# Walking the columns of the 256-column products in runs of four: two transformer blocks on one Trainium2 core

## The chip, the cores and the metric

The kernel runs on one core of one Trainium2 chip, in one launch. The metric is the device time of an execution in microseconds. Times are medians of runs; the profile is one further execution, and its own time stands beside its span in the table below.

## The reference, cut to what matters

The input is one sequence of 512 tokens with 1024 features, float32. A first block has an FFN, a token mixer (four mLSTM and four HGRN2 heads between an input projection `w_in` and an output projection) and a second FFN. A second block has a gated-linear-attention layer (GLA) and a differential-attention layer, each followed by an MLP. Every sublayer normalises its input over the features, scales and shifts it by vectors made from a condition vector, and adds its gated output to the residual `h`.

```python
def swiglu(y, w_gate, w_up, w_down):
    return (jax.nn.silu(y @ w_gate) * (y @ w_up)) @ w_down
...
y = rmsnorm(h, mix_pre_g[l]) * (1.0 + sc2) + sh2
y = token_mix(y, w_in[l], mlstm_conv_w[l], ...)
h = h + g2 * rmsnorm(y, mix_post_g[l])
...
y = jnp.square(jax.nn.relu(h @ mlp_w1[i])) @ mlp_w2[i]
x = x + gate_c * y
```

All of the large work is matrix products of 512 tokens with weights of 1024 to 4096 columns.

## The kernel before, in words

**Products.** Each operand is split into a high and a low part of type fp32r, and a product is the sum of three matmuls per 128 rows of the contraction: high by high, high by low, low by high. `fm` (L378) puts the weights into the array and streams X, so that its result has features on the partitions: lines L387 (high by high), L388 (reads the low part of X) and L389. `tm` (L394) puts X into the array and streams weights; its result has tokens on the partitions: lines L405 to L407. Both take their streamed operand and their result through `runs` (L374). For 512 columns it walks them as four passes over 32 places that lie 16 elements (64 bytes) apart, four elements at each place; for any other width it leaves them as they are.

**X.** The input X of a sublayer has eight row tiles of 128 features, each with a high and a low part of 512 tokens. Two row tiles, four parts, lie in one buffer (in the instruction order `XAr0_2048_103`, `XAr2048_2048_104`, `XAr4096_2048_105`, `XAr6144_2048_106`, and XB likewise). `to_X` (L467) makes one half of the tokens: for each of the four buffers PE transposes four blocks of `y` (L474), ACT scales and shifts them (L482, in the profile line L118), and DVE writes the high part (L486) and the low part (L487). `y` comes from `scaled_to` (DVE L460, and ACT), behind the root of the mean square (POOL L428).

**Halved stages.** In five places, at the start of a sublayer, the first products are made for tokens 0 to 255 and then for 256 to 511 (HALVES): twice in `fm_split` (L830; the mixer, first stage here, and GLA, third), three times at the start of `ffn` (L601; the second FFN, second stage here, and the two MLPs, fourth and fifth). A product there has 256 columns and 24 matmuls. Per half there are 4 products in `fm_split`, 6 in `ffn`. The first half of X is complete when the stage begins. The second is made during it: `flush` (L572) is called inside `fm` when a set number of products (`due`) has been recorded, 2 in `fm_split`, 5 or 4 in `ffn`, and writes the steps of `to_X` there, so that the first half's other products stand behind them in the program. The transposes are tied behind the last product recorded (`behind`).

```python
        if len(products) == due[0]:
            flush((1, 1, 1, 1))
...
            hi, lo = (X.groups[kp][:, i:i + 3:2, hs] for i in range(2))
            V.tensor_copy(hi, v2)
            V.tensor_tensor(lo, v2, hi.bitcast(F32), op=ALU.subtract)
```

**Order.** Each engine runs its instructions in the order that a scheduler fixes when the program is built. It works from the dependences that it finds between the places which instructions read and write, and puts in the waits between engines.

**Background.** The vectors of the condition are worked out on DVE (L247, L251) between the rest; weights come on SP's queue and are split by ACT (L338, in the profile L118) and DVE (L341). In `last_half` (L543), at the end, the last piece of the last row block is made as two `tm` products of 256 columns.

Of the kernel before, what the change touches and what calls it, by code (L numbers as in the profile page):

```python
# [35 lines left out]
def kernel(ctx: ExitStack, tc: tile.TileContext, a: dict, out: bass.AP):  # L36
# [336 lines left out]

    def runs(ap):  # L374

        return ap.rearrange("p (a b c) -> p b a c", b=4, c=4) if ap.shape[1] == 512 else ap

    def fm(p, wt, X, span, c=0):  # L378

        s, n = span  # L380
        kn = wt.shape[2]
        work(0.65 * kn * n / 512)
        for k in range(kn):
            xh, xl = X[k]
            wh, wl = wt[:, 0, k, c:c + 128], wt[:, 1, k, c:c + 128]
            xh, xl = runs(xh[:, s:s + n]), runs(xl[:, s:s + n])
            PE.matmul(runs(p), lhsT=wh, rhs=xh, start=k == 0, stop=False)  # L387
            PE.matmul(runs(p), lhsT=wh, rhs=xl, start=False, stop=False)  # L388
            done = PE.matmul(runs(p), lhsT=wl, rhs=xh, start=False, stop=k == kn - 1)  # L389
        products.append(done)  # L390
        if len(products) == due[0]:
            flush((1, 1, 1, 1))
# [1299 lines left out]
```

## Time and profile before

| | |
|---|---|
| median of 3 runs | 2275.97 us (2275.53 to 2278.2) |
| profiled execution, its own time | 2276.14 us |
| its span | 2274.4 us |
| mean granted clock of TensorE | 0.997 of 2.4 GHz |
| PE busy | 2222.1 us (98%) |
| DVE, ACT, POOL busy | 1396.7, 923.7, 189.5 us |

The span goes from the first to the last instruction of the profiled execution; its own time is 1.7 us longer. PE's busy time counts a matmul from its start to its modelled end; neighbours overlap, so that the pace of matmuls is read from their starts or their number in a window. PEld is the weight load of a matmul. A window's row gives, per engine, the busy time and the number of instructions in it, then the granted clock of TensorE. In a timeline row, the brackets tell how long the engine had been idle and what released it.

### The profile page before, as it was taken

To read this page: it belongs to the slowest core of one execution; us is meant where nothing else is said; L and a number is where in the kernel's file an instruction comes from. 1 tells how busy PE (TensorE), PEld (TensorE's weight loads), DVE (VectorE), ACT (ScalarE), POOL (GpSimd) and SP (SyncE) were. 2 spreads that over 40 slices of the span, in tenths; PEclk is the share of its full clock that TensorE was granted. 3 is DMA by queue.
4 is the path that set the end of the run, shared out by engine and by line. 5 is a ranking of instruction groups with operands and counts; after the bars stand their busy time and mean duration, and the time that the engine had idled before them with its cause. 6 is when DMAs were issued, how large, how long until landed. Compare 5 with 4: busy or idle time off the path is not lost.

```text
span 2274.4 us, 27957 instructions
## 1 busy us (share of the span) xinstructions
PE 2222.1 (98%) x10904; PEld 1837.6 (81%) x10904; DVE 1396.7 (61%) x2371; ACT 923.7 (41%) x1722; POOL 189.5 (8%) x126
## 2 busy tenths in 40 slices
PE   6999999999899999999999999999999999999998
PEld 4888887888788888888888888888886767988887
DVE  7856555765777745545644775666756577634465
ACT  4332224644665332224644443222445456433223
POOL 0111121000101111100010011101000110100000
PEclk9999999999999999999999999999999999999999
DMA  9755444445323644542332255454331321423221
GB/s 274 245 177 179 163 158 71 106 107 107 102 75 110 207 165 167 176 139 66 125 125 91 72 176 185 158 164 142 129 124 58 116 65 57 157 93 102 93 94 64
DMA packets 212900, 294.69 MB, mean 130 GB/s; under 512 B 7257, under 2 KB 120328, under 8 KB 212768
## 3 DMA queue, kind: packets, MB, share of 16 engines
q1 hardware_dynamic: 212128, 291.85, 41.4%
q8 instruction: 85, 1.39, 0.2%
q10 hardware_dynamic: 640, 1.07, 0.1%
q14 instruction: 47, 0.39, 0.1%
HBM read 290.78 MB, written 2.11 MB: 129 GB/s over the span
## 4 chain that ended last, share of the span: by engine, by line
PE 88%; DVE 5%; ACT 4%; issue 2%; POOL 1%; DMA 1%; POOLq 0%; ACTq 0%; DVEq 0%
PE PS L407 13%; PE PS L405 13%; PE PS L387 13%; PE PS L388 13%; PE PS L406 13%; PE PS L389 13%; PE PS L1498 1%; ACT RS L118 1%; DVE w L341 1%; POOL sm L428 1%; PE PS L924 1%; PE PS L1527 1%; ACT tmp L118 1%; ACT w L118 1%; DVE h L513 1%
## 5 line engine op out<-in xcount | busy, mean ns | idle before, releaser
L341 DVE TENSOR_TENSOR w<-raw,w 128x1024 fp32r<-128x1024 f32 (+1 forms) x392 | 459.9, 1177 | 405.3 <-ACT w L118 400.9
L118 ACT ACTIVATE w<-raw 128x1024 fp32r<-128x1024 f32 (+1 forms) x392 | 389.2, 1000 | 493.6 <-PE PS L407 275.8
L388 PE MATMUL PS<-XAr,w 128*128 128x512 f32 (+1 forms) x1328 | 482.2, 364 | 0.6 <-DVE XAr L713 0.5
L389 PE MATMUL PS<-XAr,w 128*128 128x512 f32 (+1 forms) x1328 | 481.0, 363 | 0.0
L387 PE MATMUL PS<-XAr,w 128*128 128x512 f32 (+1 forms) x1328 | 479.7, 365 | 0.0
L405 PE MATMUL PS<-w,XAr 128*128 128x512 f32 x806 | 313.4, 389 | 1.0 <-DVE XAr L850 0.8
L406 PE MATMUL PS<-w,XAr 128*128 128x512 f32 x806 | 311.2, 386 | 0.0
L407 PE MATMUL PS<-w,XAr 128*128 128x512 f32 x806 | 309.9, 385 | 0.0
L388 PEld LDWEIGHTS PS<-XAr,w 128*128 128x128 f32 x1328 | 250.0, 188 | 40.2 <-DVE XAr L713 1.3
L387 PEld LDWEIGHTS PS<-XAr,w 128*128 128x128 f32 x1328 | 249.5, 188 | 40.4 <-ACT XAr L118 1.4
L389 PEld LDWEIGHTS PS<-XAr,w 128*128 128x128 f32 x1328 | 250.0, 188 | 38.4
L407 PE MATMUL PS<-w,XBr 128*128 128x512 f32 x704 | 274.5, 390 | 0.5 <-DVE XBr L850 0.5
L406 PE MATMUL PS<-w,XBr 128*128 128x512 f32 x704 | 274.3, 390 | 0.0
L405 PE MATMUL PS<-w,XBr 128*128 128x512 f32 x704 | 274.2, 390 | 0.1
L118 ACT ACTIVATE tmp<-PS 128x512 f32<-128x512 f32 (+3 forms) x227 | 104.5, 466 | 407.3 <-PE PS L389 321.5
L251 DVE SCALAR_TENSOR_TENSOR acc<-araw,silu_c,acc 128x512 f32<-128x512 f32 x266 | 199.1, 748 | 40.9 <-DMA araw<-in_ada_w_dram 37.9
L261 POOL PARTITION_ALL_REDUCE tmp<-acc x38 | 131.3, 3456 | 942.9 <-DVE acc L251 791.8
L405 PEld LDWEIGHTS PS<-w,XAr 128*128 128x128 f32 x806 | 151.3, 188 | 30.3 <-DVE XAr L850 1.0
L407 PEld LDWEIGHTS PS<-w,XAr 128*128 128x128 f32 x806 | 151.2, 188 | 29.8 <-issue 0.8
L406 PEld LDWEIGHTS PS<-w,XAr 128*128 128x128 f32 x806 | 151.3, 188 | 29.0 <-issue 1.6
L405 PEld LDWEIGHTS PS<-w,XBr 128*128 128x128 f32 x704 | 131.8, 188 | 29.4 <-ACT RS L118 0.5
L406 PEld LDWEIGHTS PS<-w,XBr 128*128 128x128 f32 x704 | 132.0, 188 | 29.0 <-DVE w L341 1.0
(293 smaller groups left out, 2486.8 us busy)
## 6 DMA issues: line engine op xcount, KB each, us to landing
araw<-in_ada_w_dram SPq DMA_DIRECT2D x152, 512.0 KB
raw<-in_mlp_w_dram SPq DMA_DIRECT2D x56, 1024.0 KB
raw<-in_ffn_w_gate_dram SPq DMA_DIRECT2D x20, 1024.0 KB
raw<-in_ffn_w_up_dram SPq DMA_DIRECT2D x20, 1024.0 KB
raw<-in_ffn_w_down_dram SPq DMA_DIRECT2D x20, 1024.0 KB
raw<-in_w_in_dram SPq DMA_DIRECT2D x16, 1024.0 KB
raw<-in_gla_w_in_dram SPq DMA_DIRECT2D x12, 1024.0 KB
raw<-in_diff_w_in_dram SPq DMA_DIRECT2D x12, 1024.0 KB
```

What stands on the lines that cost most here:

```text
L118: ins = S.activation(out, in_, func, **kw)
L251: i = V.scalar_tensor_tensor(acc, raw[:, k, :], col, acc, op0=ALU.mult, op1=ALU.add)
L261: G.partition_all_reduce(red, acc, channels=128, reduce_op=bass_isa.ReduceOp.add)
L341: ins = V.tensor_tensor(wt[:, 1, ks], src[:, ks], wt[:, 0, ks].bitcast(F32), op=ALU.subtract)
L387: PE.matmul(runs(p), lhsT=wh, rhs=xh, start=k == 0, stop=False)
L388: PE.matmul(runs(p), lhsT=wh, rhs=xl, start=False, stop=False)
L389: done = PE.matmul(runs(p), lhsT=wl, rhs=xh, start=False, stop=k == kn - 1)
L405: PE.matmul(runs(p), lhsT=xh[:, s:s + 128], rhs=wh, start=n == 0, stop=False)
L406: PE.matmul(runs(p), lhsT=xh[:, s:s + 128], rhs=wl, start=False, stop=False)
L407: done = PE.matmul(runs(p), lhsT=xl[:, s:s + 128], rhs=wh, start=False, stop=n == last)
L428: G.tensor_tensor(r, ms, mhalf[:, 0:w], op=ALU.pow)
L513: V.scalar_tensor_tensor(h[:, blk, C2[c]], y[blk][:, C2[c]], r[:, b:b + 1], h[:, blk, C2[c]], op0=ALU.mult, op1=ALU.add)
```

## The change

`runs` now walks operands and results of 256 columns too: four passes over 16 places, 64 bytes apart, four elements at each.

```diff
     def runs(ap):
 
-        return ap.rearrange("p (a b c) -> p b a c", b=4, c=4) if ap.shape[1] == 512 else ap
+        return ap.rearrange("p (a b c) -> p b a c", b=4, c=4) if ap.shape[1] >= 256 else ap
```

It is reached by the products of the five halved stages, and by the two of 256 columns in `last_half`. The scheduled order changes with it in the five stages.

First place: PE, first halved stage, where the second half's transposes (L474) are followed by the rest. `w_2787` and `w_2792` hold the weights of the third and fourth product of the first half; `waits DVE_49` is a wait for DVE. Before, the third product is over and the fourth is three quarters through:

```order
L389 MATMUL PS_70<-XAr4096_2048_105,w_2792 128x256 [waits DVE_49]
L387 MATMUL PS_70<-XAr4096_2048_105,w_2792 128x256
L388 MATMUL PS_70<-XAr4096_2048_105,w_2792 128x256
L389 MATMUL PS_70<-XAr4096_2048_105,w_2792 128x256
L474 MATMUL PS_70<-ident_113,Y_111 128x128 [waits DVE_49]
L474 MATMUL PS_70<-ident_113,Y_111 128x128
L387 MATMUL PS_70<-XAr6144_2048_106,w_2792 128x256
L474 MATMUL PS_70<-ident_113,Y_111 128x128 [waits DVE_49]
L474 MATMUL PS_70<-ident_113,Y_111 128x128 x5
L388 MATMUL PS_70<-XAr6144_2048_106,w_2792 128x256
```

The same place with the change:

```order
L387 MATMUL PS_70<-XAr0_2048_103,w_2787 128x4x16x4 [waits Activation_49]
L387 MATMUL PS_70<-XAr0_2048_103,w_2792 128x4x16x4 [waits Activation_49]
L474 MATMUL PS_70<-ident_113,Y_111 128x128 [waits DVE_49] x2
L474 MATMUL PS_70<-ident_113,Y_111 128x128 x6
L474 MATMUL PS_70<-ident_113,Y_111 128x128 [waits Activation_49]
L474 MATMUL PS_70<-ident_113,Y_111 128x128 x3
L388 MATMUL PS_70<-XAr0_2048_103,w_2787 128x4x16x4 [waits DVE_49]
L474 MATMUL PS_70<-ident_113,Y_111 128x128 [waits Activation_49]
L474 MATMUL PS_70<-ident_113,Y_111 128x128 x3
L389 MATMUL PS_70<-XAr0_2048_103,w_2787 128x4x16x4
L387 MATMUL PS_70<-XAr0_2048_103,w_2787 128x4x16x4 [waits DVE_49]
```

All but the first matmul of each of the two products have moved behind the transposes, and L388 and the second L387 wait for DVE: for the buffer's second half, which they do not read.

Second place: DVE, third halved stage, where the second half is written (L486, L487); one piece of the difference, - before, + now.

```order
-L486 CAST XAr_2048_103<-RS 128x2x256 [waits Activation_49]
-L251 SCALAR_TENSOR_TENSOR acc<-araw,silu_c_399,acc 128x512 [waits DVE_49]
+L341 TENSOR_TENSOR w<-raw,w 128x1024 [waits DMAHW0_49,Activation_49]
+L486 CAST XAr_2048_103<-RS 128x2x256 [waits PE_49,Activation_49]
+L486 CAST XAr_2048_104<-RS 128x2x256 [waits PE_49,Activation_49]
 L487 TENSOR_TENSOR XAr_2048_103<-RS,XAr_2048_103 128x2x256 [waits DVE_49]
-L486 CAST XAr_2048_104<-RS 128x2x256 [waits Activation_49]
-L486 CAST XAr_2048_105<-RS 128x2x256 [waits Activation_49]
 L487 TENSOR_TENSOR XAr_2048_104<-RS,XAr_2048_104 128x2x256 [waits DVE_49]
+L486 CAST XAr_2048_105<-RS 128x2x256 [waits PE_49,Activation_49]
+L251 SCALAR_TENSOR_TENSOR acc<-araw,silu_c_399,acc 128x512
 L487 TENSOR_TENSOR XAr_2048_105<-RS,XAr_2048_105 128x2x256 [waits DVE_49]
```

Each L486 now waits for PE as well, as it does in all five stages, and the weight split L341 has come ahead of the first of them.

## Rows read from the trace of the kernel before

**Rows 1.** The page, parts 1 and 4: busy times; the chain that ended last.

```profile
PE 2222.1 (98%) x10904; PEld 1837.6 (81%) x10904; DVE 1396.7 (61%) x2371; ACT 923.7 (41%) x1722; POOL 189.5 (8%) x126
...
PE 88%; DVE 5%; ACT 4%; issue 2%; POOL 1%; DMA 1%; POOLq 0%; ACTq 0%; DVEq 0%
```

**Rows 2.** Groups by line and form, PE: count, busy us, mean ns of one.

```profile
L388 PE MATMUL PS<-XAr,w 128*128 128x512 f32 x1008 | 392.1, 389 | 0.5 <-DVE XAr L713 0.5
...
L388 PE MATMUL PS<-XAr,w 128*128 128x256 f32 x320 | 90.0, 283 | 0.2 <-DVE XAr L487 0.2
...
L387 PE MATMUL PS<-XBr,w 128*128 128x256 f32 x96 | 27.0, 281 | 0.0
...
L405 PE MATMUL PS<-w,XAr 128*128 128x256 f32 x12 | 3.4, 280 | 0.0
```

**Rows 3.** Windows inside dense stretches: us, busy (x instructions) per engine, PEclk, DMA.

```profile
728.00:738.00 10.00, 10.00 (x87) 10.00 (x86) 6.66 (x7) 3.38 (x5) 4.01 (x1) 1.00 0.88 272
...
842.00:862.00 20.00, 20.00 (x90) 16.54 (x90) 12.39 (x17) 6.26 (x8) 3.23 (x1) 1.00 0.61 207
```

**Rows 4.** Timeline of PE, first halved stage: start, us, instruction, idle before.

```profile
398.77 0.28 PE L387 MATMUL PS<-XAr,w 128*128 128x256 f32 x1
...
411.03 0.44 PE L474 MATMUL PS<-ident,Y 128*128 128x128 f32 x2 [1.42 <-DVE Y L460]
...
425.66 0.28 PE L389 MATMUL PS<-XAr,w 128*128 128x256 f32 x1
```

**Rows 5.** Timeline of DVE, first halved stage.

```profile
413.52 0.69 DVE L487 TENSOR_TENSOR XAr<-RS,XAr 128x512 fp32r<-128x512 f32 x1
...
416.71 0.69 DVE L487 TENSOR_TENSOR XAr<-RS,XAr 128x512 fp32r<-128x512 f32 x1
```

**Rows 6.** Timeline of PE, third halved stage.

```profile
1070.15 0.28 PE L387 MATMUL PS<-XAr,w 128*128 128x256 f32 x1
...
1080.98 0.44 PE L474 MATMUL PS<-ident,Y 128*128 128x128 f32 x2 [1.64 <-DVE Y L460]
...
1096.62 0.28 PE L389 MATMUL PS<-XAr,w 128*128 128x256 f32 x1
```

**Rows 7.** Timeline of ACT and of DVE, third halved stage.

```profile
1084.74 1.09 ACT L118 ACTIVATE w<-raw 128x1024 fp32r<-128x1024 f32 x1
...
1086.68 1.22 DVE L341 TENSOR_TENSOR w<-raw,w 128x1024 fp32r<-128x1024 f32 x1
...
1088.70 0.63 DVE L487 TENSOR_TENSOR XAr<-RS,XAr 128x512 fp32r<-128x512 f32 x1
```

**Rows 8.** Timeline of PE, second, fourth and fifth halved stage.

```profile
718.00 1.04 PE L474 MATMUL PS<-ident,Y 128*128 128x128 f32 x8
...
740.12 0.28 PE L389 MATMUL PS<-XAr,w 128*128 128x256 f32 x1
...
1309.79 1.04 PE L474 MATMUL PS<-ident,Y 128*128 128x128 f32 x8
...
1334.55 0.28 PE L389 MATMUL PS<-XAr,w 128*128 128x256 f32 x1
...
1930.90 1.04 PE L474 MATMUL PS<-ident,Y 128*128 128x128 f32 x8
...
1955.58 0.28 PE L389 MATMUL PS<-XBr,w 128*128 128x256 f32 x1
```

**Rows 9.** Timeline of DVE, second, fourth and fifth halved stage.

```profile
724.03 1.28 DVE L487 TENSOR_TENSOR XAr<-RS,XAr 128x512 fp32r<-128x512 f32 x2
...
1315.52 0.69 DVE L487 TENSOR_TENSOR XAr<-RS,XAr 128x512 fp32r<-128x512 f32 x1
...
1937.90 0.69 DVE L487 TENSOR_TENSOR XBr<-RS,XBr 128x512 fp32r<-128x512 f32 x1
```

**Rows 10.** Timeline of PE, one wait in the mixer; the window over it.

```profile
579.52 3.62 PE L924 MATMUL PS<-tmp 128*128 128x128 f32 x16 [6.13 <-DVE tmp L952]
...
576.00:583.00 7.00, 3.48 (x17) 3.51 (x18) 5.51 (x16) 2.84 (x4) 0.20 (x1) 0.51 0.00 0
```

## Prediction

> **What bounds the kernel now.** I read the page first. TensorE (PE) is busy 98% of the span and carries 88% of the chain that ended last [rows 1]: what is added ahead of its next matmul, or taken off a matmul, reaches the end nearly whole. Then the groups of PE by line and form [rows 2] tell how much work the edit touches. In `fm` (L387 to L389) there are 320 matmuls of 256 columns on each of the three lines from XA and 96 on each from XB, so 3 x 416 = 1248; in `tm` (L405 to L407) 3 x 12 = 36. That is 1284 of 10904. The mean in a group is one instruction's latency, not its pace: for the pace I took windows inside dense stretches [rows 3]. 87 matmuls of 256 contiguous columns touch 10.00 us, so one follows another in (10.00 + 0.28)/87 = 118 ns; 90 of 512 walked columns touch 20.00 us, (20.00 + 0.39)/90 = 226.6 ns. Per column that is 0.461 against 0.443 ns.
>
> The timelines of the five places where `fm` works on halves of 256 tokens come next. There PE multiplies the first half of X while ACT and DVE still make the second half, and then transposes that half (L474). The 36 of `tm` are the last of the kernel and touch no such place.
>
> **The change, part by part.** Beside the walk itself, the order of the instructions moves (the section on the change shows it). The compiler's dependence tracking takes a walk over columns 0 to 255 of an X tile as touching what is written to columns 256 to 511. So L486 now waits for PE in the five second halves; and, what matters, first-half products written behind `flush()` wait on DVE for second-half tiles that they never read. They used to cover PE while that half was made. Time of the DVE work itself: unchanged, since the products that L486 waits for stand ahead of the transposes and are over before. PE is what waits.
>
> *First halved stage* (`fm_split` in the mixer). From 398.77 us PE ran 90 matmuls (counted in the order) and stood 1.42 us until DVE's L460 released the transposes at 411.03 [rows 4]. Now only 50 stand ahead of them, which end near 398.8 + 50 x 0.118 = 404.7 us; PE then stands some 6.3 us, since L460 does not hang on them. The last tile of the second half leaves DVE at 416.71 + 0.69 = 417.4 [rows 5]. Of the 192 matmuls of the stage 118 stand behind the wait for it, so the last ends its turn at 417.5 + 118 x 0.118 = 431.4. Before it was 425.66 + 0.12 = 425.8 [rows 4]. **+5.6 us.** What fits between is the 24 other matmuls, whose tiles come at DVE's pace.
>
> *Third stage* (GLA's `fm_split`). Again 50 ahead where 77 stood: they end at 1070.15 + 5.9 = 1076.1, the transposes come at 1080.98 [rows 6], so PE stands 4.9 us. The last tile is ready at 1088.70 + 0.63 = 1089.3 [rows 7]; DVE's L341 of 1.22 us and ACT's weight copy of 1.09 us [rows 7] move from before the last tile to before the first, which lies ahead of the last either way. 106 matmuls are left: 1089.4 + 12.5 = 1101.9 against 1096.62 + 0.12 = 1096.7. **+5.2 us**; were ACT's copy, now ahead of all eight scalings, late by its own length, 1.1 more.
>
> *Second, fourth, fifth stage* (the FFNs). The transposes start where they did, behind 120, 96 and 96 matmuls [rows 8], and only the products behind them now wait. Last tile and matmuls left: 724.03 + 1.28 = 725.3 [rows 9], 135; 1316.2, 162; 1938.6, 161. With 0.1 us from DVE to PE and 118 ns each they end at 741.3, 1335.4 and 1957.7, against 740.2, 1334.7 and 1955.7 [rows 8]. **+1.1, +0.7, +2.0 us.** Sum of the five: **+14.6 us**.
>
> *The clock.* Where PE once stood 6.13 us for DVE's L952, the window from 576 to 583 us has a granted clock of 0.51 (1.2 GHz) [rows 10]. A stand of 6.3 us and one of 4.9 us are new. At half clock the 3.48 us that PE was busy there would have been about 1.7. I take **+2 us** for two falls: much of the slow stretch lies under the waits. Bounds: 0 (no fall) and 7 (two stretches of 7 us, wholly busy).
>
> *The walk.* No row has 256 walked columns. What is ahead of a wait does not count: 118 + (120 + 135) + 106 + (96 + 162) + (96 + 161) + 36 = 1030 matmuls do. The lower bound is half of the same lines' walked 512, 113.3 ns. The upper: that row's excess over its columns, 226.6 - 213.3 (512 at 2.4 GHz) = 13.3 ns, is wholly per instruction, so 106.7 + 13.3 = 120 ns. I take 114.5, near the first, since line, tiles and walk are the same and only its length is halved, and some of an instruction's cost stays: 1030 x 3.5 ns = **-3.6 us** (-4.8 to +2.1). The page "TensorE: Matmul & The Clock Gate" of the Trainium skill, section "Back-to-back issue gap", has 256 warm columns issue every 109 ns in whatever order; the 118 ns here do not agree, and if a walk recovered all of that, the term would be -9.3 us and the sum 2283.4. No run here shows it.
>
> Copies, weight splits, DMAs and instruction counts stay; nothing moves on POOL, on SP two waits for ACT are added ahead of weight loads that PE does not stand for.
>
> *Sum:* against the profiled execution, 2276.14 us (span 2274.4; the median of the runs is 2275.97): 2276.14 + 14.6 + 2.0 - 3.6 = **2289.1 us**.
>
> **The rivals.**
> - *The stage's loss is absorbed behind it: not slower.* Between the first halved stage and the next stands the one long wait of PE, 6.13 us [rows 10]. If DVE came to L952 when it does now, PE would arrive 5.6 us later and wait so much less, and its clock would not fall there (1.7 us): 2289.1 - 5.6 - 1.7, with the walk at 113.3 another 1.2: 2280.6, within 0.2%. It decides once DVE's road to L952 is free of the halved products. Against it: f, q and k of the heads are those products' sinks, so DVE starts later as well. 0.12.
> - *The added waits are met already: faster.* If tiles were there when PE comes, the walk alone would count, 1284 x 4.7 ns = 6 us: 2270.1. The transposes themselves wait for L460 (1.42 and 1.64 us idle [rows 4, 6]), which speaks against it. 0.07.
> - *The walk is dearer at 256.* Sixteen places come around sooner than thirty-two. If a pass costs the excess of the walked 512 on top of today's 118 ns: 131.3, 1030 x 13.3 = +13.7 us and 2306.4. The page "PSUM — Partial Sum Buffer" of the Trainium skill, section "Specifications (TRN2)", says that any non-contiguous access slows matmuls significantly; by that rule this rival holds. The rows speak against the rule for runs of four: 0.443 ns a column walked, 0.461 not [rows 3]. 0.06.
> - *The clock falls hard:* +7 in place of 2, 2294.1; part of the forecast's range.
>
> **How the numbers follow.** The forecast (the five waits) has 0.75. A change of 0.2%, 4.6 us, is about what a measurement of this kernel tells from none. The forecast's low end is the walk at 113.3 ns and no fall of the clock, 2276.1 + 14.6 - 4.8 = 2285.9; its high end, ACT late by 1.1, clock +7 and walk +2.1, is 2300.9, all at once unlikely, so 2298. To hold 8 in 10 the range takes in the absorbing rival too: 2279 to 2298. Slower: 0.75 + 0.06 = 0.81; same: the absorbing rival and 0.01 of the next, 0.13; faster: the rest of that one, 0.06.
>
> **What would show it.** Right: in the first halved stage the transposes start near 411 us behind some 6 us of idle PE, the stage lasts 5 to 6 us longer; the third likewise; L388 or L389 is released by DVE's L486 or L487; dense windows of 256 columns show 113 to 116 ns. Wrong: no idle of PE over 2 us before L474 there, or a dense pace of 118 ns or more, or a granted clock that stays at 1.00 with the loss still whole.

## The result, and the profile after

The change made the kernel slower: 2290.07 us (median of 4 runs, 2289.32 to 2291.63) against 2277.09 us for the kernel before, run beside it (2275.53 to 2279.29). The ratio is 1.0061, 95% interval 1.0049 to 1.0073. The forecast was 2289.1 us, 13.0 above the 2276.14 it started from; the measured time is 13.0 above that of the kernel run beside it.

The page after, parts 1 and 4, corresponds to [rows 1]. PE is as busy as before, in a span that is 13.2 us longer:

```profile
span 2287.6 us, 27975 instructions
...
PE 2223.1 (97%) x10904; PEld 1836.6 (80%) x10904; DVE 1394.6 (61%) x2371; ACT 924.2 (40%) x1722; POOL 190.5 (8%) x126
...
PE 88%; DVE 5%; ACT 3%; issue 2%; POOL 1%; DMA 1%; POOLq 0%; ACTq 0%; DVEq 0%
```

The waits of PE after (waiting line, releasing line: us in all, times, longest):

```profile
PE PS L474 <- DVE Y L460: 14.0, 5, 6.3
PE PS L924 <- DVE tmp L952: 6.5, 2, 5.7
...
PE PS L474 <- ACT RS L118: 4.2, 8, 0.8
...
PE PS L388 <- DVE XBr L486: 1.3, 1, 1.3
PE PS L388 <- DVE XAr L486: 1.1, 1, 1.1
```

The same view of the kernel before has the first three of these lines with other sums:

```profile
PE PS L924 <- DVE tmp L952: 6.8, 2, 6.1
...
PE PS L474 <- DVE Y L460: 5.9, 5, 1.6
...
PE PS L474 <- ACT RS L118: 1.3, 4, 0.8
```

They show two things. The transposes L474 stood 5.9 us for L460 and now stand 14.0. L460 is not later: in the first stage the transposes start 12.2 us after the first product, 12.3 before (rows below and [rows 4]). PE comes earlier, since the products that covered the time have gone behind the transposes. And L388, which in both these places belongs to a product of the first half, now waits for L486, which writes the second.

The timeline of PE after corresponds to [rows 4, 6, 8]:

```profile
397.55 0.27 PE L387 MATMUL PS<-XAr,w 128*128 128x256 f32 x1
...
409.71 2.15 PE L474 MATMUL PS<-ident,Y 128*128 128x128 f32 x8 [6.27 <-DVE Y L460]
...
430.12 0.28 PE L389 MATMUL PS<-XAr,w 128*128 128x256 f32 x1
...
725.88 0.38 PE L388 MATMUL PS<-XAr,w 128*128 128x256 f32 x1 [1.10 <-DVE XAr L486]
...
1075.68 0.27 PE L387 MATMUL PS<-XAr,w 128*128 128x256 f32 x1
...
1086.50 1.97 PE L474 MATMUL PS<-ident,Y 128*128 128x128 f32 x8 [4.93 <-DVE Y L460]
...
1095.98 0.27 PE L387 MATMUL PS<-XAr,w 128*128 128x256 f32 x1
...
1108.01 0.28 PE L389 MATMUL PS<-XAr,w 128*128 128x256 f32 x1
```

The first stage goes from 397.55 to 430.12, 32.57 us, where [rows 4] give 425.66 - 398.77 = 26.89; the third takes 32.33 us against 26.47 [rows 6]. These two are 5.7 and 5.9 us longer. The timeline of DVE after, first and third stage, shows that the second half is made hardly later within its stage: the last tile leaves 415.85 + 0.69 - 397.55 = 19.0 us behind the first product of stage one, 18.6 before [rows 4, 5], and 19.2 as before in stage three [rows 6, 7].

```profile
415.85 0.69 DVE L487 TENSOR_TENSOR XAr<-RS,XAr 128x512 fp32r<-128x512 f32 x1
...
1088.73 1.22 DVE L341 TENSOR_TENSOR w<-raw,w 128x1024 fp32r<-128x1024 f32 x1
...
1094.21 0.62 DVE L487 TENSOR_TENSOR XAr<-RS,XAr 128x512 fp32r<-128x512 f32 x1
```

What is left to multiply behind that tile is more: in the program 118 and 106 matmuls of the two stages stand behind the wait for it. In the first stage PE reaches the first of the 118 as the tile comes (416.60 against 416.54). In the third it is late: the tile leaves at 1094.83, the first of the 106 starts only at 1095.98, and ten more matmuls are still to come ahead of it. Windows of the change, to set beside [rows 3] and the half-clock window of [rows 10]:

```profile
406.70:413.50 6.80, 3.54 (x15) 2.92 (x16) 4.66 (x9) 4.67 (x11) 1.18 (x2) 0.50 1.00 258
...
1086.00:1092.80 6.80, 5.57 (x25) 4.87 (x26) 6.73 (x13) 6.06 (x11) 0.68 (x1) 0.50 0.71 229
...
1330.00:1346.00 16.00, 16.00 (x142) 16.00 (x141) 12.59 (x18) 8.99 (x17) 4.37 (x1) 1.00 0.27 70
```

The first two are new stretches at 1.2 GHz (granted clock 0.50). They begin inside the two long stands, which end at 409.71 and 1086.50, and go on behind them. The third lies in the second half of stage four, where nothing but products of 256 columns run: 142 matmuls touch 16 us, (16.00 + 0.28)/142 = 114.6 ns each. The same piece of the kernel before has 137, 118.8 ns:

```profile
1318.00:1334.00 16.00, 16.00 (x137) 16.00 (x137) 12.30 (x17) 8.77 (x17) 4.37 (x1) 1.00 0.24 71
```

So the walk did shorten each matmul, by some 4 ns, and the waits took more than it gave. This 16 us window, in each kernel at about the same place of stage four, is the measure of the pace below; one matmul more or less in it is 0.8 ns. It is one place of ten: read from start to start in the first and the second half of every stage, plain columns take 117.3 to 118.7 ns, the walk 114.3 to 115.6. The measure of a stage is the time from the start of its first product to the start of its last.

### The profile page after: what moved, and what is told of

Read it like the earlier page. It is cut to its first block, busy times and chain, and to the rows that moved or that the text cites. A ratio compares the mean times of both kernels' runs of the same rounds, so it can differ in the third digit from the quotient of the medians.

```text
span 2287.6 us, 27975 instructions
## 1 busy us (share of the span) xinstructions
PE 2223.1 (97%) x10904; PEld 1836.6 (80%) x10904; DVE 1394.6 (61%) x2371; ACT 924.2 (40%) x1722; POOL 190.5 (8%) x126
## 4 chain that ended last, share of the span: by engine, by line
PE 88%; DVE 5%; ACT 3%; issue 2%; POOL 1%; DMA 1%; POOLq 0%; ACTq 0%; DVEq 0%
PE PS L388 14%; PE PS L387 14%; PE PS L389 13%; PE PS L407 13%; PE PS L405 13%; PE PS L406 13%; PE PS L1498 1%; ACT RS L118 1%; DVE w L341 1%; PE PS L924 1%; POOL sm L428 1%; PE PS L1527 1%; ACT tmp L118 1%; ACT w L118 1%; PE PS L474 0%
## 5 line engine op out<-in xcount | busy, mean ns | idle before, releaser
L341 DVE TENSOR_TENSOR w<-raw,w 128x1024 fp32r<-128x1024 f32 (+1 forms) x392 | 457.3, 1171 | 407.9 <-ACT w L118 403.2
L388 PE MATMUL PS<-XAr,w 128*128 128x512 f32 (+1 forms) x1328 | 480.9, 363 | 1.6 <-DVE XAr L486 1.1
L387 PE MATMUL PS<-XAr,w 128*128 128x512 f32 (+1 forms) x1328 | 477.5, 363 | 0.0
L388 PEld LDWEIGHTS PS<-XAr,w 128*128 128x128 f32 x1328 | 250.5, 189 | 41.2 <-DVE XAr L486 1.6
L387 PEld LDWEIGHTS PS<-XAr,w 128*128 128x128 f32 x1328 | 249.2, 188 | 40.5 <-ACT XAr L118 1.4
L251 DVE SCALAR_TENSOR_TENSOR acc<-araw,silu_c,acc 128x512 f32<-128x512 f32 x266 | 199.1, 748 | 38.7 <-DMA araw<-in_ada_w_dram 35.9
```

The source lines that it names most:

```text
L251: i = V.scalar_tensor_tensor(acc, raw[:, k, :], col, acc, op0=ALU.mult, op1=ALU.add)
L341: ins = V.tensor_tensor(wt[:, 1, ks], src[:, ks], wt[:, 0, ks].bitcast(F32), op=ALU.subtract)
```

## Experiments

Ratios are to the kernel before, run beside each on the same chip. The first four separate waits from walk.

### 1. The walk without the waits

The high part of two row tiles is one write that spans, from its first to its last address, the low part of the first tile and the first half of the second tile. If that span is what the dependence tracking takes a read of 64 short runs to touch, a write for each row tile must free the products. It did: the order on PE is that of before but for 58 of 10904 places, the walk stays.

```diff
-            hi, lo = (X.groups[kp][:, i:i + 3:2, hs] for i in range(2))
-            V.tensor_copy(hi, v2)
-            V.tensor_tensor(lo, v2, hi.bitcast(F32), op=ALU.subtract)
+            for kk in range(2):
+                hi, lo = (X.groups[kp][:, 2 * kk + i, hs] for i in range(2))
+                V.tensor_copy(hi, v2[:, kk, :])
+                V.tensor_tensor(lo, v2[:, kk, :], hi.bitcast(F32), op=ALU.subtract)
```

> The change as it is, but DVE writes each row tile's second half by an instruction of its own (L486 and L487 of 256 columns, twice as many), so that no write spans from one row tile into the next and the first-half products lose their waits for the second half. Theory (the loss was those waits; the walk gains 4 ns on each of 1284 matmuls): 5.1 us less than before, some 0.7 of it ahead of the waits for L460 and so lost, 2272.5 us where before is 2277 (ratio 0.998); PE stands under 2.5 us before the transposes of the first and the third halved stage, and the clock stays at full there. Rival (the walk or what it does to the clock costs by itself): 2285 us or more, whatever the waits. Second rival (split writes make the last tile late by what the walk gains): 2276 to 2278 us.

Measured: 2274.01 us against 2276.15, ratio 0.9993 (0.9984 to 1.0002). The 16 us window has 142 matmuls, as the change has, and PE stands 1.68 us in the first stage and 1.81 in the third before the transposes:

```profile
411.55 0.44 PE L474 MATMUL PS<-ident,Y 128*128 128x128 f32 x2 [1.68 <-DVE Y L460]
```

Without the waits the 13 us are gone; the rival that the walk itself costs falls. The gain is smaller than expected, and by stage one sees where: stages three to five are 0.5, 0.9 and 0.7 us shorter than before, but the second is 0.7 longer. The timeline of DVE there (the split moves L486 and L487 to L487 and L488):

```profile
721.84 0.29 DVE L487 CAST XAr<-RS 128x256 fp32r<-128x256 f32 x1
722.90 0.75 DVE L251 SCALAR_TENSOR_TENSOR acc<-araw,silu_c,acc 128x512 f32<-128x512 f32 x1 [0.77 <-DMA araw<-in_ada_w_dram]
723.57 0.42 DVE L488 TENSOR_TENSOR XAr<-RS,XAr 128x256 fp32r<-128x256 f32 x1
...
726.46 0.75 DVE L488 TENSOR_TENSOR XAr<-RS,XAr 128x256 fp32r<-128x256 f32 x2
```

The last tile is done at 727.21, 23.1 us into the stage; before it was done 21.6 us into it. Two things stand in these rows: twice as many instructions, of 0.29 and 0.42 us, and a background step (L251) that waits 0.77 us for its DMA between them, which it does not in the kernel before.

### 2. The split writes alone

The same edit of the writes on the kernel before, columns in plain order.

> The kernel before with the split writes alone, columns of 256 products in plain order. Theory (the split costs nothing that PE waits for): within 1.5 us of before, matmuls of 256 columns 118 ns apart. Rival (each of the 64 extra DVE instructions of the five stages delays the last tile by some 0.1 us, eight on the way to each last tile): 3 to 4 us slower than before.

Measured: 2276.45 us, ratio 1.0003 (0.9994 to 1.0011); 137 matmuls in the window. The time is within what was expected. By stage, the second is 1.8 us longer and the others within 0.1 us; so the split has a price, in one stage, that the whole time hardly shows.

### 3. All first-half products ahead of the second half's steps

```diff
-        due[0] = len(products) + 2
+        due[0] = len(products) + 4
```

> The change as it is, but in the two stages of fm_split all four products of the first half (96 matmuls) are written ahead of the steps that make the second half, not two, so that the added waits have nothing to hold up there; the FFN stages keep theirs. Theory: the first and the third stage come back to their length of before or 0.5 us under it, the FFN stages keep their +2.4 us, the end its -0.2: 2277 + 2 = 2279 us (2278 to 2280.5), no PE stand over 2 us before the transposes and no half clock there. Rival (the loss is the walk's or comes from DVE waiting for PE, not PE's wait for DVE): 2287 us or more.

Measured: 2283.17 us, ratio 1.0031 (1.0019 to 1.0044): half the loss came back, not all that was expected. The first stage is still 2.4 us longer than before, the third 1.7. The timeline of PE, first stage:

```profile
410.51 1.38 PE L474 MATMUL PS<-ident,Y 128*128 128x128 f32 x8 [1.10 <-DVE Y L460]
413.95 0.65 PE L474 MATMUL PS<-ident,Y 128*128 128x128 f32 x4 [2.07 <-ACT RS L118]
...
416.21 0.41 PE L387 MATMUL PS<-XAr,w 128*128 128x256 f32 x1
416.43 0.41 PE L388 MATMUL PS<-XAr,w 128*128 128x256 f32 x1
```

My theory had left out that the first-half products cover two gaps, the one ahead of the transposes and the one behind the first eight of them. With all 96 ahead, the second gap is bare (2.07 us), and behind it matmuls start 213 ns apart, at half clock. The second stage, whose order is the change's, fell to half clock as well (granted clock 0.50 from 726.2 to 728.7) and took 1.6 us more than in the change, and the third fell too (0.50 from 1090.8 to 1094.0). All of this is in the 5 us by which the expectation missed.

### 4. The waits without the walk

The kernel before, columns in plain order, with a dependence put in by hand from each first-half product behind `flush` to the second half's writes of its buffer, so that PE has the order and the waits of the change (lines move by 6 to 12). DVE and ACT, too, run in the change's order; DVE's waits for PE are left out.

```diff
+            if tails and span == (0, 256):
+                held(*((first, tails[k // 2][1]) if k % 2 else (second, tails[k // 2][0])))
```

> The kernel before, its 256-column products in plain order, with the change's waits put in by hand: a first-half product written behind flush waits for the second half's writes of its pair of row tiles, as in the change; on PE the order and the waits of the five stages are those of the change. Theory (waits and walk are two separate terms): the change's 2290.1 us plus the walk's gain behind the waits, about 1030 x 4 ns = 4.1 us: 2294 us (2292.5 to 2296), ratio 1.0078; matmuls of 256 columns 118 ns apart. Rival (the loss needs the walk, for instance DVE waiting for PE, which is left out here): 2277 to 2280 us. Rival (the walk gains nothing on the path): 2290 us.

Measured: 2291.30 us against 2275.32, ratio 1.0072 (1.0060 to 1.0085); 137 matmuls in the window. The time is below the range expected, because the kernel before was 1.8 us faster beside it; the ratio covers the 1.0078. The stand is nearly the change's (6.06 against 6.27 us), and the first and the third stage last as long as there or longer:

```profile
397.46 0.28 PE L393 MATMUL PS<-XAr,w 128*128 128x256 f32 x1
...
409.61 2.15 PE L482 MATMUL PS<-ident,Y 128*128 128x128 f32 x8 [6.06 <-DVE Y L468]
...
430.68 0.28 PE L395 MATMUL PS<-XAr,w 128*128 128x256 f32 x1
...
1076.30 0.28 PE L393 MATMUL PS<-XAr,w 128*128 128x256 f32 x1
...
1109.16 0.28 PE L395 MATMUL PS<-XAr,w 128*128 128x256 f32 x1
```

The waits, with the order that they bring, make the whole loss and a little more. The intervals of this run and of the change overlap, so the walk's gain does not show in the two times; the stages show it. Differences to the kernel before, us:

| stage | waits and walk (the change) | waits alone | walk alone (split writes) | the prediction's wait term |
|---|---|---|---|---|
| first | +5.7 | +6.3 | -0.2 | +5.6 |
| second | +0.7 | +1.1 | +0.7 | +1.1 |
| third | +5.9 | +6.4 | -0.5 | +5.2 |
| fourth | +0.2 | +0.9 | -0.9 | +0.7 |
| fifth | +1.5 | +2.2 | -0.7 | +2.0 |
| last two products | -0.2 | 0.0 | -0.2 | 0 |
| sum | +13.8 | +16.9 | -1.8 | +14.6 |

The difference of the first two columns, 3.1 us, is what the walk gives back behind the waits. Each column is one profile. Between the profiles of kernels whose order in a stage is that of before, the second stage differs by up to 0.5 us and the first and third by 0.2: the entries of the second stage are hardly clear of that.

### 5. Where the pace comes from: the length and distance of the runs

Four other walks. With 4 and with 32 runs the compiler finds no dependence between the halves, even with the writes of before, and the order on PE, DVE and ACT is that of before; with the change's 64 runs it does. Two places 128 columns apart with 64 elements at each, on the change:

```diff
-        return ap.rearrange("p (a b c) -> p b a c", b=4, c=4) if ap.shape[1] >= 256 else ap
+        b, c = (2, 64) if ap.shape[1] == 256 else (4, 4)
+        return ap.rearrange("p (a b c) -> p b a c", b=b, c=c) if ap.shape[1] >= 256 else ap
```

> The 256-column products walked in two passes over two places 128 columns apart, 64 elements at each: not the plain order either, but the writes are as before (two row tiles in one instruction) and the compiler finds no dependence between the halves. Theory (waits come only with the many short runs, and so does the pace): matmuls of 256 columns 117 to 119 ns apart, time within 1 us of before. Rival (any order other than the plain one gives the pace): 114 ns and 2272 us. Rival by the page 'PSUM — Partial Sum Buffer' of the Trainium skill (any non-contiguous access slows matmuls): over 120 ns and 2279 us or more.

Measured: 2276.48 us, ratio 1.0002 (0.9993 to 1.0011), 137 matmuls in the window: the time and the pace of before, as the theory had it.

Runs of 8, sixteen places 64 bytes apart (`b, c = (2, 8)`):

> The 256-column products walked in two passes over sixteen places 64 bytes apart, 8 elements at each: 32 runs instead of 64, the order of the program is that of before and no first-half product waits for the second half. Theory A (what makes a matmul shorter is that the places lie 64 bytes apart): 114 to 115 ns from one to the next, 1284 x 3.5 ns less = 2272 us (ratio 0.998). Theory B (it is the runs of four): 117 to 119 ns and within 1 us of before. If waits came with any short runs, PE would stand 5 us or more before the transposes of the first stage: not expected.

Runs of 8, eight places 128 bytes apart (`b, c = (4, 8)`):

> The same in four passes over eight places 128 bytes apart, 8 elements at each, again 32 runs without the added waits. Theory A (places 64 bytes apart): 117 to 119 ns and the time of before. Theory B (runs of four): the same 118 ns. A third (four passes, whatever the run): 114 ns and 2272 us.

Measured: 2275.36 us, ratio 0.9995 (0.9986 to 1.0004), and 2274.83 us, ratio 0.9992 (0.9983 to 1.0001). Their windows, in this order (one fence for each kernel):

```profile
1317.00:1333.00 16.00, 16.00 (x140) 16.00 (x139) 12.14 (x17) 8.98 (x17) 4.37 (x1) 1.00 0.25 69
```

```profile
1317.00:1333.00 16.00, 16.00 (x136) 16.00 (x135) 12.59 (x17) 8.34 (x16) 4.37 (x1) 1.00 0.28 79
```

116.3 and 119.7 ns. For the second of the two this window is not typical. Its last 101 matmuls of stage two start from 727.91 to 739.46, 115.5 ns apart, where plain columns take 117.3:

```profile
727.91 0.27 PE L388 MATMUL PS<-XAr,w 128*128 128x256 f32 x1
...
739.46 0.28 PE L389 MATMUL PS<-XAr,w 128*128 128x256 f32 x1
```

Read in this way in both halves of every stage, runs of 8 take 116.7 to 118.0 ns at 64 bytes; at 128 bytes 115.5 to 115.9 in the first three stages and the first half of the fourth, 120.0 in the second half of the fourth and 117.4 in the fifth. Neither theory A nor theory B covers this: runs of 8 lie between the two paces or, in places, on the slow one, and differ from stage to stage.

Runs of four at twice the distance, eight passes over eight places 128 bytes apart, with split writes (`b, c = (8, 4)`; 64 runs):

> Split writes as in the first experiment; 256 columns walked in eight passes over eight places 128 bytes apart, four elements at each, in place of sixteen places 64 bytes apart. Runs of 8 gave 118 ns at 64 bytes and 115 at 128 bytes. Theory C (the distance from one run to the next counts, and 64 bytes with runs of four already have all of it): 114 ns and the time of the first experiment, 2274 us. Theory D (the farther the shorter): 112 ns or less, 2272 us. If it is the number of passes that costs: 116 ns or more.

Measured: 2279.48 us, ratio 1.0018 (1.0009 to 1.0027), 136 matmuls in the window, 119.7 ns, and 102 in 12 us in stage two, 120.4 ns. Theories C and D both fall: short runs alone don't make the pace, and walked this way they are slower than the plain order. Of the walks tried, only runs of four 64 bytes apart gave 114 to 116 ns in every stage. Why is open.

### 6. Operand or result

Split writes, and only one side of the products of `fm` walked.

```diff
+        rp = runs if span[1] == 512 else (lambda ap: ap)
...
-            PE.matmul(runs(p), lhsT=wh, rhs=xh, start=k == 0, stop=False)
+            PE.matmul(rp(p), lhsT=wh, rhs=xh, start=k == 0, stop=False)
```

> Split writes as in the first experiment; in the 256-column products of fm only the operand is walked in runs of four, the result is written in plain order (its tokens are permuted, so the values are not the reference's). If the gain comes from reading the operand: 114 ns in fm; if from writing the result: 118 ns. Theory: 114 ns would go with the operand's reads; I give that 0.4. No stand over 2.5 us before the transposes either way.

> Split writes; in the 256-column products of fm only the result is walked, the operand is read in plain order (tokens permuted as well). If the gain comes from writing the result: 114 ns; if from reading the operand: 118 ns. I give the result's side 0.6.

Measured: operand alone 2274.62 us, ratio 0.9991 (0.9982 to 1.0000); result alone 2276.66 us, ratio 1.0003 (0.9993 to 1.0012). The windows of the first and of the second:

```profile
1318.00:1334.00 16.00, 16.00 (x142) 16.00 (x141) 12.54 (x18) 8.99 (x17) 4.37 (x1) 1.00 0.26 69
```

```profile
1318.00:1334.00 16.00, 16.00 (x137) 16.00 (x136) 12.92 (x18) 8.19 (x15) 4.37 (x1) 1.00 0.29 83
```

All of the gain lies on the operand's side: 114.6 ns with the operand walked, 118.8 with the result walked, which is the plain pace. I had given the result's side 0.6 and was wrong. That a walked result costs nothing speaks, for this walk, against the rule of the Trainium skill's page "PSUM — Partial Sum Buffer", section "Specifications (TRN2)", that any non-contiguous access slows matmuls significantly.

### 7. PE kept busy in its stands

The change, with matmuls that nobody reads in the stands of the first and third stage.

```diff
+            if pad[0]:
+                products[-1] = spare(44)
             flush((1, 1, 1, 1))
+            if pad[0]:
+                spare(16)
```

> The change as it is, with matmuls of 256 plain columns of X's first half into a spare bank, whose result nobody reads, in PE's two stands of fm_split: 44 (5.2 us) ahead of the transposes, 16 more behind them. They depend on nothing that is late. Theory (the two half-clock stretches of the change cost 0.5 us in the first stage and 0.95 us in the third): the clock stays at 1.00 in both, and the time falls by 1.4 us to 2288.7 (2287.7 to 2289.5). As predicted before the change ran, 2 us: 2288.1. Rival (clock costs nothing on the path, since the tiles pace PE): 2290 us. Rival (the filler stands in the way of the tiles' matmuls): 2291 us or more.

Measured: 2292.33 us, ratio 1.0076 (1.0062 to 1.0089), not faster than the change. The windows show that the clock was held at full in both places:

```profile
406.70:413.50 6.80, 5.46 (x43) 4.82 (x43) 4.98 (x10) 5.31 (x13) 1.18 (x2) 1.00 1.00 269
...
1086.00:1092.80 6.80, 6.10 (x46) 5.22 (x46) 6.22 (x11) 5.27 (x10) 0.47 (x1) 1.00 0.79 243
```

The last tile of stage one came sooner, and PE could not use it:

```profile
412.97 1.07 PE L394 MATMUL PS<-XAr,w 128*128 128x256 f32 x7
413.88 0.28 PE L387 MATMUL PS<-XAr,w 128*128 128x256 f32 x1
```

The last seven filler matmuls (L394) run until the first waiting matmul starts at 413.88. In the change the first had started at 412.88 and the third at 413.95. From there PE is busy without a gap. The stage is 0.2 us longer than the change's, the third 0.8, and the fifth 1.6 us, with a stretch at half clock (0.50 from 1947.2 to 1950.5) that the change's profile has not. So the filler stood in the way, as the last rival said, and the run does not tell what the half clock cost the change.

### 8. Only where it gains

Walk and split writes in the third to fifth stage and in the last two products, the first two stages as before.

> The walk in runs of four with split writes in the third, fourth and fifth halved stage and in the last two products alone; the first two stages, where the split writes of the first experiment came late (the second was 0.7 us longer than before), stay as before. Theory: the stages' gains of the first experiment add up, 0.5 + 0.9 + 0.7 + 0.2 = 2.3 us less than before, ratio 0.9990 (0.9980 to 0.9997). Rival (a gain in a stage is taken back behind it): 1.0000.

Measured: 2274.84 us against 2276.48, ratio 0.9993 (0.9984 to 1.0003). The three stages and the end gain 0.6, 1.0, 0.7 and 0.2 us, about as in the first experiment; the first two, in plain order, were 0.2 and 0.5 us longer than in the profile of before. The interval holds what was expected and also 1.0000: this version was not shown to be faster than the kernel before.

## Why the prediction was right, step by step

- **The waits, +14.6 us.** Right in kind and, nearly, in size. The experiment with the waits alone prices them, with the clock they bring, at +16.9 us where the prediction had 14.6 + 2 = 16.6. The stages without a long stand came as forecast: second +1.1 (1.1), fourth +0.9 (0.7), fifth +2.2 (2.0). The working behind them, last tile plus the matmuls left behind it, holds in these three.
- **First and third stage.** +6.3 and +6.4 with the waits alone, 0.7 and 1.2 us over their terms of 5.6 and 5.2. The stands were forecast at 6.3 and 4.9 us and are 6.27 and 4.93. In both stages the clock fell to half during them. In the first, with the waits alone, the last tile comes 0.4 us later in the stage than before, and PE reaches it 0.3 us after it came. The third stage's term took PE to be at the wait for the last tile when the tile comes. It was not: the tile was done at 1094.83 and the first matmul behind it started 1.15 us later (1.2 with the waits alone). PE had no gap from 1090.88 on; with 36 matmuls of the earlier tiles ahead of it, and up to 1092.79, at half clock, they started some 215 ns apart. An estimate from these figures: 114.6 ns apart the 36 would have been over at 1095.0, so about 1 us of the lateness goes with the clock. DVE's L341 (1.22 us, at 1088.73) does stand ahead of the first tile there, as the prediction read from the order. It did not make the last tile late; the first it did, and so it has a part in when PE could begin.
- **The clock, +2 us.** Two stretches at half clock are there. The 1.9 us by which those two stages exceed their terms is the size that was taken, and the estimate for the third stage fits it, but the experiment that held the clock up did not give it back: that all of it is the clock's price was not shown. What one stretch can cost is seen in the last section, 1.4 us.
- **The walk, -3.6 us.** The pace is 114.6 ns (114.5 taken). The gain behind the waits is 3.1 us by the stages. The page "TensorE: Matmul & The Clock Gate" of the Trainium skill, section "Back-to-back issue gap", has 262 cycles, 109 ns, for 256 warm columns, as the gap of a matmul by itself; in a stream with weight loads, it says, both set the spacing. Neither order reaches 109 ns here.
- **The rivals.** *Loss absorbed behind the first stage*: no. PE's longest wait at L924 went from 6.13 us [rows 10] to 5.7, but the time from the first stage's last product to the second stage's first did not shrink: 278.1 us before, 278.5 with the change, 278.1 with the waits alone. That wait is no measure of it: with the split writes alone, where nothing is lost in the first stage, its longest is 4.7. The loss goes through, as was argued. *Waits met already*: no, PE stands 14.0 us for L460. *Walk dearer at 256*: no, though a walk of eight passes was (119.7 ns). *The clock falls hard*: no, nothing near 7 us.
- **The sum.** By stage the change added 13.8 us, and 0.6 between the stages; the spans differ by 13.2. The rest lies ahead of the first stage, which starts 1.2 us earlier, at 397.55 against 398.77: the profile of the kernel before has a stretch at half clock there, where PE ran 10 matmuls in place of 19, and the change's has none. The first row is of the kernel before:

```profile
29.90:33.30 3.40, 3.40 (x10) 2.55 (x9) 2.43 (x6) 0.12 (x1) 0.00 (x0) 0.50 1.18 293
```

```profile
29.90:33.30 3.40, 3.40 (x19) 2.79 (x19) 2.98 (x10) 0.46 (x1) 0.00 (x0) 1.00 1.18 293
```

- **Luck.** The edit does not reach that place, and not every profile has such a stretch, so single profiles compare to about 1 us only. The parts agree with the forecast no better than that; that the whole agrees to a tenth is chance.

## What to carry to other kernels

A change of access pattern is a change of the dependences that a compiler can see: compare the order of the instructions before pricing the pattern, and look for reads that now wait for writes to places they never touch. Price such a wait from the last producer: when it is done, and how many matmuls stand behind it. Ask also whether the engine will be there by then: in the third stage PE came 1.15 us late. The idle time that appears ahead of the wait is no second cost, but the clock that falls in it can be. Work that covers a gap may cover a second one behind it (the third experiment): moving it to the first bares the second.

## What the runs showed that was not expected

The pace of a 256-column matmul depends on how its operand is read and not on how its result is written: 114 to 116 ns with the operand in runs of four 64 bytes apart, 117 to 119 in plain order, 120 to 123 in runs of four 128 bytes apart.

The same stand does not always bring the clock down. In the third stage PE stood 1.81 us for L460 in the first experiment and 1.82 us with the operand alone walked. The window from 1083 to 1086 us, the first experiment first:

```profile
1083.00:1086.00 3.00, 3.00 (x28) 2.92 (x27) 2.96 (x9) 3.00 (x8) 0.00 (x0) 1.00 1.00 325
```

```profile
1083.00:1086.00 3.00, 3.00 (x17) 3.00 (x15) 2.96 (x10) 1.93 (x5) 0.00 (x0) 0.52 0.95 315
```

At half clock 17 matmuls ran where 28 did, and that stage was 1.4 us longer (27.4 against 25.9).

Where one write spans two row tiles, an operand of 64 runs was taken as touching the other half, one of 32 runs was not.
